# A decoder block with a product-key expert layer on one core: the low halves of split operands issued later, the high halves earlier, part of the one-hot scaling on another engine, and more gathered rows in the first expert product

## The chip, the cores and the metric

One NeuronCore of one Trainium2 chip runs the whole program in one launch. The metric is device microseconds of that core, the median of several runs.

## The reference, cut to what matters

```
x = x + (sigmoid(gate_a) * conv_branch + sigmoid(gate_b) * attention_branch) @ w_out
h = rmsnorm(x)                                   # 512 tokens x 1024
q = h @ peer_wq                                  # 8 heads x two halves of 128
s1, s2 = scores of the two halves against 128 keys each
top 16 of each half, the 256 sums, their top 16  # 16 experts per head and token
experts = e1 * 128 + e2                          # 128 of 16384 experts per token
gates = softmax of the 16 scores
out = sum over the 128 experts: gelu(h . u[expert]) * gate * v[expert]
return rmsnorm(x + out)
```

Everything is float32, and the result has to hold float32 accuracy.

## The kernel before, in words

The kernel multiplies in TensorE's rounded float32 format. Every operand is split in two: a high half, rounded by ScalarE (a copy into that format), and a low half, which is operand minus high half, by VectorE. `mm3` then issues three matmuls for each product: low x high, high x low, high x high.

The program runs in stages; the two of this change are the last two, the **expert products**. For 384 of the 512 tokens (three tiles of 128) the kernel doesn't gather experts. It computes all 16384 of them densely, in 128 blocks of 128 experts:

- **First product** (`u_block`, one call for each block b): `pu[b]` (128 x 1024) times the 384 normalised tokens `hden`, 24 matmuls of 384 columns, then a gelu by ScalarE out of PSUM into `gel`, which is stored to HBM as `Sd` two blocks at a time (the last eight blocks stay on chip as `kept`).
- **Second product** (the last loop over b): `pv[b]` times the weighted gelu values, 18 matmuls of 512 columns into six PSUM banks that stay open for all 128 blocks. For each pair of blocks `a_pair` reloads `Sb` from HBM, VectorE multiplies it by the dense gate matrix `G`, and the product is split into `ah` (ScalarE) and `al` (VectorE).

For the remaining 128 tokens the experts are gathered: for each of 128 slots, POOL gathers one row of `pu` for each token (an indirect DMA of 128 rows x 4 KB) and VectorE takes a dot product (`gathered`, 128 "dots" rows); then 128 rows of `pv` follow, each of which VectorE scales and adds into `x`. These 256 **rows** run beside the two products: so many in the first, the rest spread evenly over the second.

Beside the first product runs the **routing**, all of it background work on VectorE: `level1` (top 16 of every key score, `top16`, five instructions for each of 64 lists), `level2` (candidate sums, their top 16, the expert numbers; one call for each tile of 128 tokens, with round trips through ScalarE), and `scatter` (for the three dense tiles: one-hot matrices by comparison, which PE multiplies into the gate matrix `G`, 16 groups of 8 tokens for each tile). A group needs an `ohs` tile with four parts: a one-hot of the second key (part 0), of the first key (part 1), part 1 times the high half of the gate (part 2, VectorE), and part 1 times the low half (part 3, eight small ScalarE copies with a scale, L1067). PE's 16 small matmuls for a group are queued by `later` behind some block and evicted by two ScalarE copies (`gst`, L1079).

Three things set the order of the work around the change. The engines' queues are written out in program order: nothing reorders them. The weights come through `pump`: three raw buffers (`WRAW`), four split pairs (`WSPL`). `next_w`, called at the start of block b, flushes what is pending (it issues the high and the low half of block b+2's weight), starts a raw load (SP's queue), and leaves block b+3's weight pending. And the background work after each block of the first product is dealt out in nominal microseconds: `bgrun` runs the routing until `U_DVE - U_BG` is spent (`U_DVE` alone until the first tile's experts are known; `U_SC` more when a group of matmuls was queued), then the rows until `U_BG` is spent.

```
        while state["split"] < min(n_split, len(stream)):
            ...
            pend.append([stream[i][1], lo, raw, hi, 0, 0])
```

```
        room = U_DVE
        if len(later) > busy:
            later.pop(0)()
            room += U_SC
        share = U_BG if ready else 0.0
        busy = bgrun(room - share, bgr)
        more = busy or later
        if ready:
            bgrun(share if more else U_END, bgg)
```

The lines that the text below names: L127 and L131 are `flush` (high half `whi` on ScalarE, low half `wlo` on VectorE), L141 the raw load, L172 to L174 the three matmuls, L1110 a dots row, L1116 a row of the second kind, L1151 the gelu, L1192 the multiplication by `G`, L206 and L208 the two halves `ah` and `al` in `split`.

## Time and profile before

| | us |
|---|---|
| median of 3 runs (lowest to highest) | 1809.54 (1803.93 to 1812.57) |
| the profiled execution | 1810.52 |
| its span, first to last instruction | 1808.5 |
| PE busy | 1767.8 |
| VectorE (DVE) busy | 1507.4 |
| ScalarE (ACT) busy | 877.3 |
| DMA, over the span | 239 GB/s |
| first expert product (PE, 126 blocks) | 671 to 1257 |
| second expert product (PE) | 1257 to 1799 |

Matmuls are pipelined, so the time that PE is "busy" covers gaps of up to the length of one matmul: how fast a stage runs is read from the distance between two starts. An engine's wait is put down to the one that released it last. Idle time of an engine that nobody waits for costs nothing.

### The profile page before, as it was taken

To read this page: it belongs to the slowest core of one execution; us is meant where nothing else is said; L and a number is where in the kernel's file an instruction comes from. 1 tells how busy PE (TensorE), PEld (TensorE's weight loads), DVE (VectorE), ACT (ScalarE), POOL (GpSimd) and SP (SyncE) were. 2 spreads that over 40 slices of the span, in tenths; PEclk is the share of its full clock that TensorE was granted. 3 is DMA by queue.
4 is the path that set the end of the run, shared out by engine and by line. 5 is a ranking of instruction groups with operands and counts; after the bars stand their busy time and mean duration, and the time that the engine had idled before them with its cause. 6 is when DMAs were issued, how large, how long until landed. Compare 5 with 4: busy or idle time off the path is not lost.

```text
span 1808.5 us, 25395 instructions
## 1 busy us (share of the span) xinstructions
PE 1767.8 (98%) x9289; PEld 1538.4 (85%) x9289; DVE 1507.4 (83%) x2649; ACT 877.3 (49%) x1622; POOL 388.0 (21%) x303
## 2 busy tenths in 40 slices
PE   8999999999999999999999999999999999999997
PEld 7887777788888889999999999999787787787786
DVE  5799999998755699999888987766888888888887
ACT  5665665535524323344488499953333333333333
POOL 0000000000000000023322322143443444454440
PEclk9999999999999999999999999999999999999999
DMA  6332222122343125578989899999999999999994
GB/s 224 97 94 72 86 76 80 61 82 93 117 148 129 63 78 161 180 250 286 312 277 319 313 314 320 318 355 408 369 384 382 372 385 380 378 384 373 373 335 147
DMA packets 164477, 432.92 MB, mean 239 GB/s; under 512 B 13696, under 2 KB 63488, under 8 KB 162304
## 3 DMA queue, kind: packets, MB, share of 16 engines
q1 hardware_dynamic: 111840, 239.37, 38.5%
q0 software_dynamic: 39424, 138.43, 21.6%
q10 hardware_dynamic: 13088, 53.50, 7.8%
q8 instruction: 73, 1.20, 0.3%
q14 instruction: 52, 0.43, 0.1%
HBM read 376.20 MB, written 50.86 MB: 236 GB/s over the span
## 4 chain that ended last, share of the span: by engine, by line
PE 50%; DVE 22%; ACT 12%; DMA 10%; issue 5%; ACTq 0%; POOL 0%; SPq 0%; POOLq 0%; DVEq 0%
PE mm L172 15%; PE mm L173 15%; PE mm L174 15%; DMA wraw<-in_pv 7%; DVE wlo L131 5%; DVE x L1116 5%; DVE y L498 5%; ACT whi L127 4%; ACT ohs L1067 2%; DMA wraw<-in_pu 2%; ACT ah L206 2%; DVE Sb L1192 2%; PE pvp L1076 2%; DVE grow L1110 2%; DVE ptl L637 1%
## 5 line engine op out<-in xcount | busy, mean ns | idle before, releaser
L131 DVE TENSOR_TENSOR wlo<-wraw,whi 128x1024 fp32r<-128x1024 f32 (+1 forms) x434 | 432.8, 1005 | 101.3 <-ACT whi L127 97.1
L127 ACT ACTIVATE whi<-wraw 128x1024 fp32r<-128x1024 f32 (+1 forms) x429 | 373.7, 893 | 94.6 <-DMA wraw<-in_pv 38.8
L172 PE MATMUL mm<-h2h,wlo 128*128 128x384 f32 (+1 forms) x1152 | 397.8, 345 | 2.1 <-DVE wlo L131 1.6
L173 PE MATMUL mm<-h2l,whi 128*128 128x384 f32 (+1 forms) x1152 | 392.8, 341 | 0.5 <-DVE h2l L208 0.5
L174 PE MATMUL mm<-h2h,whi 128*128 128x384 f32 (+1 forms) x1152 | 393.0, 341 | 0.0
L1097 POOL DMA_INDIRECT grow<-in_pur,sx x128 | 179.1, 1399 | 613.8 <-DVE grow L1110 369.1
L1097 POOL DMA_INDIRECT grow<-in_pv,sx x128 | 185.9, 1452 | 230.1 <-DVE x L1116 203.4
L172 PEld LDWEIGHTS mm<-h2h,wlo 128*128 128x128 f32 x1152 | 216.8, 188 | 7.6 <-DVE wlo L131 2.0
L173 PEld LDWEIGHTS mm<-h2l,whi 128*128 128x128 f32 x1152 | 217.1, 188 | 5.7 <-DVE h2l L208 1.1
L174 PEld LDWEIGHTS mm<-h2h,whi 128*128 128x128 f32 x1152 | 216.8, 188 | 5.3
L173 PE MATMUL mm<-wlo,ah 128*128 128x512 f32 x512 | 203.4, 397 | 9.4 <-DVE wlo L131 9.0
L172 PE MATMUL mm<-whi,al 128*128 128x512 f32 x512 | 199.9, 390 | 0.2 <-DVE al L208 0.2
L174 PE MATMUL mm<-whi,ah 128*128 128x512 f32 x512 | 199.7, 390 | 0.0
L206 ACT ACTIVATE ah<-Sb 128x768 fp32r<-128x768 f32 x60 | 50.8, 846 | 303.9 <-DVE Sb L1192 254.5
L498 DVE SCALAR_TENSOR_TENSOR y<-z,cw,y 128x512 f32<-128x512 f32 x240 | 174.2, 749 | 1.1 <-ACT y L495 0.2
L1116 DVE SCALAR_TENSOR_TENSOR x<-grow,dots,x 128x1024 f32<-128x1024 f32 x128 | 164.5, 1285 | 1.1
L172 PE MATMUL mm<-hTh,wlo 128*128 128x512 f32 x384 | 161.3, 420 | 3.2 <-DVE qa L570 1.7
L1110 DVE SCALAR_TENSOR_TENSOR grow<-grow,hd 128x1024 f32<-128x1024 f32 x128 | 155.0, 1217 | 0.7 <-DMA grow<-in_pur,sx 0.7
L174 PE MATMUL mm<-hTh,whi 128*128 128x512 f32 x384 | 150.6, 392 | 0.0
L173 PE MATMUL mm<-hTl,whi 128*128 128x512 f32 x384 | 150.0, 391 | 0.0
L1151 ACT ACTIVATE gel<-mm 128x384 f32<-128x384 f32 x118 | 57.7, 489 | 182.4 <-PE mm L174 110.1
L173 PEld LDWEIGHTS mm<-wlo,ah 128*128 128x128 f32 x512 | 96.0, 188 | 41.9 <-DVE wlo L131 23.0
(284 smaller groups left out, 2943.9 us busy)
## 6 DMA issues: line engine op xcount, KB each, us to landing
wraw<-in_pu SPq DMA_DIRECT2D x128, 512.0 KB, 4.9
wraw<-in_pv SPq DMA_DIRECT2D x128, 512.0 KB, 6.4
wraw<-in_w_ct SPq DMA_DIRECT2D x48, 512.0 KB, 3.5
Gd<-gst SPq DMA_DIRECT2D x24, 1024.0 KB, 9.8
G<-Gd ACTq DMA_DIRECT2D x16, 1536.0 KB, 10.0
Sb<-Sd ACTq DMA_DIRECT2D x60, 384.0 KB, 6.6
Sd<-gel SPq DMA_DIRECT2D x59, 384.0 KB, 6.1
wraw<-in_w_q SPq DMA_DIRECT2D x16, 512.0 KB, 3.5
```

Source lines behind the costliest of these rows:

```text
L127: nc.scalar.activation(hi[:, nh * q:hi_to * q], raw[:, nh * q:hi_to * q], AF.Copy)
L131: eng.tensor_tensor(lo[:, c], raw[:, c], hi[:, c].bitcast(F32), op=ALU.subtract)
L172: nc.tensor.matmul(o, ll, rh, start=first, stop=False)
L173: nc.tensor.matmul(o, lh, rl, start=False, stop=False)
L174: nc.tensor.matmul(o, lh, rh, start=False, stop=last)
L206: nc.scalar.activation(hi, src, AF.Copy, scale=1.0 if scale is None else scale)
L498: dve.scalar_tensor_tensor(acc, z[:, w:w + S], cw[:, j, w:w + 1], acc, op0=ALU.mult, op1=ALU.add)
L1067: nc.scalar.activation(o[:, 3, g, :, t], o[:, 1, g, :, t], AF.Copy, scale=gl32[:, t0 + u:t0 + u + 1])
L1097: pool.indirect_dma_start(out=t, out_offset=None, in_=src, in_offset=bass.IndirectOffsetOnAxis(ap=sx[:, n % NG:n % NG + 1], axis=0))
L1110: yield 1.25, dve.scalar_tensor_tensor(t, t, 1.0, hd, op0=ALU.mult, op1=ALU.mult, accum_out=dots[:, k:k + 1])
L1116: yield 1.28, dve.scalar_tensor_tensor(o, t, dots[:, k:k + 1], o, op0=ALU.mult, op1=ALU.add)
L1151: nc.scalar.activation(gel[c][:, n, :], p[:, :TD], AF.Gelu_apprx_tanh)
```

## The change

Six edits, all in the two expert products:

- `u_block` calls `flush(4, 0)` after its matmuls and ahead of its gelu: the high half of the weight that this block's `next_w` left pending (block b+3's) is issued there on ScalarE; its low half stays for the next `next_w`, behind this block's background work on VectorE.
- The second product calls `flush(4, 0)` right after `next_w`, to the same effect.
- In `a_pair` the low half `al` is no longer issued right behind the high half: it is put on a list, which the second product's loop runs (`a_low`) after this block's rows.
- In `scatter` the low gates are also stored in float16 (`et` has a fourth part), and one VectorE product scales the one-hots of the first four of a group's eight tokens; ScalarE keeps the other four copies.
- `U_DVE` goes from 2.9 to 3.2.
- `U_BG` goes from 1.15 to 1.3.

```diff
-U_DVE = 2.9
+U_DVE = 3.2
 U_SC = 0.8
-U_BG = 1.15
+U_BG = 1.3
...
-        et = rt.tile([P, 3, P], F16, tag="et", name="et", bufs=2)
+        et = rt.tile([P, 4, P], F16, tag="et", name="et", bufs=2)
...
+        dve.tensor_copy(et[:, 3, :], gl32)
...
-                for u in range(TB):
+                yield 0.36, dve.tensor_tensor(o[:, 3, :TB // TI // 2], o[:, 1, :TB // TI // 2],
+                                              bc(3)[:, :TB // TI // 2], op=ALU.mult)
+                for u in range(TB // 2, TB):
                     g, t = divmod(u, TI)
                     nc.scalar.activation(o[:, 3, g, :, t], o[:, 1, g, :, t], AF.Copy, scale=gl32[:, t0 + u:t0 + u + 1])
...
         p = proj(hden, False)
+        flush(4, 0)
         nc.scalar.activation(gel[c][:, n, :], p[:, :TD], AF.Gelu_apprx_tanh)
...
-        split(hi, lo, a)
+        nc.scalar.activation(hi, a, AF.Copy)
         As[k] = (hi, lo)
+        apend.append(lambda: dve.tensor_tensor(lo, a, hi.bitcast(F32), op=ALU.subtract))
+
+    apend = []
+
+    def a_low():
+        while apend:
+            apend.pop(0)()
...
         if b == NK - KEEP * SB2 + 4:
             a_pair(0)
+            a_low()
...
         hi, lo = next_w()
+        flush(4, 0)
         ah, al = As[c]
         if b == 0:
             left = 2 * NG - ngath[0]
         while 2 * NG - ngath[0] > left * (NK - 5 - b) // (NK - 4):
             if next(bgg, None) is None:
                 break
+        a_low()
```

Three places show how the instructions move. The first is VectorE in the second product, two pairs of blocks (`Sb` is the multiplication by `G`, `al` the low half of that pair, `wlo` the low half of a weight, `x` a gathered row). Before:

```order
L1192 TENSOR_TENSOR Sb<-Sb,G 128x768
L208 TENSOR_TENSOR al<-Sb,ah 128x768
L131 TENSOR_TENSOR wlo<-wraw,whi 128x1024
L1116 SCALAR_TENSOR_TENSOR x_4729<-grow,dots,x_4729 128x1024
L131 TENSOR_TENSOR wlo<-wraw,whi 128x1024
L1116 SCALAR_TENSOR_TENSOR x_4729<-grow,dots,x_4729 128x1024 x2
L1192 TENSOR_TENSOR Sb<-Sb,G 128x768
L208 TENSOR_TENSOR al<-Sb,ah 128x768
```

and now:

```order
L1196 TENSOR_TENSOR Sb<-Sb,G 128x768
L131 TENSOR_TENSOR wlo<-wraw,whi 128x1024
L1119 SCALAR_TENSOR_TENSOR x_4729<-grow,dots,x_4729 128x1024 x2
L1201 TENSOR_TENSOR al<-Sb,ah 128x768
L131 TENSOR_TENSOR wlo<-wraw,whi 128x1024
L1119 SCALAR_TENSOR_TENSOR x_4729<-grow,dots,x_4729 128x1024
L1196 TENSOR_TENSOR Sb<-Sb,G 128x768
```

Between the multiplication that feeds `ah` and the subtraction that reads it stood nothing; now a weight's low half and at least one row stand there. Over the whole program 13 of the 256 rows have moved ahead of the second product's loop: 95 stand there before, 108 now, so the loop has 161 and then 148.

The second place is VectorE in the first product during `level1`, from one weight's low half to the next but one. Before (nine instructions of routing for one weight):

```order
L131 TENSOR_TENSOR wlo<-wraw,whi 128x1024
L908 MAX v<-sc_5948 128x8
L909 MAX_INDEX ix<-v,sc_5948 128x8
L910 MATCH_REPLACE sc_5948<-v,sc_5948 128x128
L911 MAX v<-sc_5948 128x8
L912 MAX_INDEX ix<-v,sc_5948 128x8
L908 MAX v<-sc_5948 128x8
L909 MAX_INDEX ix<-v,sc_5948 128x8
L910 MATCH_REPLACE sc_5948<-v,sc_5948 128x128
L911 MAX v<-sc_5948 128x8
L131 TENSOR_TENSOR wlo<-wraw,whi 128x1024
```

and now (two whole lists, ten instructions):

```order
L131 TENSOR_TENSOR wlo<-wraw,whi 128x1024
L908 MAX v<-sc_5949 128x8
L909 MAX_INDEX ix<-v,sc_5949 128x8
L910 MATCH_REPLACE sc_5949<-v,sc_5949 128x128
L911 MAX v<-sc_5949 128x8
L912 MAX_INDEX ix<-v,sc_5949 128x8
L908 MAX v<-sc_5949 128x8
L909 MAX_INDEX ix<-v,sc_5949 128x8
L910 MATCH_REPLACE sc_5949<-v,sc_5949 128x128
L911 MAX v<-sc_5949 128x8
L912 MAX_INDEX ix<-v,sc_5949 128x8
L131 TENSOR_TENSOR wlo<-wraw,whi 128x1024
```

The first tile's experts are ready three blocks earlier, and the last group of the scatter stands one block earlier.

The third place is ScalarE during the scatter (`ohs` the scaled one-hots, `gel` the gelu, `gst` a group's eviction). Before:

```order
L1067 ACTIVATE ohs<-ohs,gl_9810 128x128 x8
L127 ACTIVATE whi<-wraw 128x1024
L1151 ACTIVATE gel<-mm 128x384
L1079 ACTIVATE gst<-pvp 128x128x4 x2
L1067 ACTIVATE ohs<-ohs,gl_9810 128x128 x8
```

and now:

```order
L1070 ACTIVATE ohs<-ohs,gl_9650 128x128 x4
L127 ACTIVATE whi<-wraw 128x1024
L1155 ACTIVATE gel<-mm 128x384
L1082 ACTIVATE gst<-pvp 128x128x4 x2
L1070 ACTIVATE ohs<-ohs,gl_9650 128x128 x4
```

A group has half the copies. The high half stands in the same place, but it is that of the weight one block further on. PE gets two groups behind the same block at 7 places before and at 4 now.

## Rows read from the trace of the kernel before

**Rows 1.** The page's first part: busy time of each engine, its share of the span, and the number of instructions.

```profile
PE 1767.8 (98%) x9289; PEld 1538.4 (85%) x9289; DVE 1507.4 (83%) x2649; ACT 877.3 (49%) x1622; POOL 388.0 (21%) x303
```

**Rows 2.** Busy time of each engine in stretches of the span: the stretch, its length, then busy time and number of instructions of PE, PE's weight loads, DVE, ACT and POOL, the granted TensorE clock as a share of 2.4 GHz, the mean busy share of the 16 DMA engines, and GB/s. The first two are the two products.

```profile
671.00:1257.00 586.00, 578.20 (x3816) 569.98 (x3815) 488.89 (x1082) 361.99 (x768) 135.58 (x98) 1.00 0.86 289
1257.00:1808.50 551.50, 532.54 (x2306) 429.20 (x2304) 472.69 (x476) 182.88 (x209) 232.03 (x162) 1.00 0.94 356
1040.00:1200.00 160.00, 155.20 (x1220) 149.91 (x1219) 126.44 (x182) 147.99 (x382) 34.19 (x28) 0.99 0.99 318
1200.00:1250.00 50.00, 48.37 (x280) 48.05 (x279) 27.60 (x37) 16.05 (x23) 18.98 (x15) 1.00 1.03 406
1262.00:1750.00 488.00, 478.81 (x2072) 385.67 (x2071) 422.42 (x416) 161.65 (x175) 217.06 (x150) 1.00 0.99 375
```

**Rows 3.** The timeline of PE in the second product: start and length in us, engine, line, operation, tiles and shapes. The first matmul of the product, two matmuls seven starts apart within a block, and the last matmul of the program.

```profile
1257.05 0.39 PE L172 MATMUL mm<-whi,al 128*128 128x512 f32 x1
...
1405.01 0.39 PE L172 MATMUL mm<-whi,al 128*128 128x512 f32 x1
...
1406.60 0.39 PE L173 MATMUL mm<-wlo,ah 128*128 128x512 f32 x1
...
1798.74 0.39 PE L174 MATMUL tp<-whi,ah 128*128 128x512 f32 x1
```

**Rows 4.** What PE waited for, in the first product (the first two rows, 675 to 1262 us) and in the second (the last row, 1262 us to the end): us in total, times, the longest.

```profile
PE pvp L1076 <- ACT gst L1079: 6.2, 13, 2.2
PE mm L172 <- DVE wlo L131: 1.6, 1, 1.6
...
PE mm L173 <- DVE wlo L131: 9.0, 21, 0.7
```

**Rows 5.** What DVE waited for in the second product (1262 to 1790 us), in the same form.

```profile
DVE al L208 <- ACT ah L206: 61.1, 63, 1.2
DVE wlo L131 <- ACT whi L127: 8.3, 9, 1.8
```

**Rows 6.** The timeline of DVE over one pair of blocks of the second product; in brackets the idle time ahead and what ended it.

```profile
1499.77 0.95 DVE L1192 TENSOR_TENSOR Sb<-Sb,G 128x768 f32<-128x768 f32 x1
1501.68 0.96 DVE L208 TENSOR_TENSOR al<-Sb,ah 128x768 fp32r<-128x768 f32 x1 [0.96 <-ACT ah L206]
1502.63 1.23 DVE L131 TENSOR_TENSOR wlo<-wraw,whi 128x1024 fp32r<-128x1024 f32 x1
1503.78 1.28 DVE L1116 SCALAR_TENSOR_TENSOR x<-grow,dots,x 128x1024 f32<-128x1024 f32 x1
...
1507.30 0.95 DVE L1192 TENSOR_TENSOR Sb<-Sb,G 128x768 f32<-128x768 f32 x1
```

**Rows 7.** PE in the first product: the first matmuls of blocks 5 and 6, from the timeline; the group of all small matmuls of the scatter (busy time, mean ns, idle time ahead); and the one of the 48 groups of 16 that waited longest, from the timeline.

```profile
684.95 0.33 PE L172 MATMUL mm<-h2h,wlo 128*128 128x384 f32 x1
...
689.11 0.33 PE L172 MATMUL mm<-h2h,wlo 128*128 128x384 f32 x1
...
L1076 PE MATMUL pvp<-ohs 128*128 128x128 f16 x768 | 52.9, 219 | 6.2 <-ACT gst L1079 6.2
...
1113.18 1.10 PE L1076 MATMUL pvp<-ohs 128*128 128x128 f16 x16 [2.25 <-ACT gst L1079]
```

**Rows 8.** The timeline of ACT over one block of the scatter (rows merged: x8 is eight copies).

```profile
941.43 1.04 ACT L127 ACTIVATE whi<-wraw 128x1024 fp32r<-128x1024 f32 x1
942.38 0.47 ACT L1151 ACTIVATE gel<-mm 128x384 f32<-128x384 f32 x1
942.75 1.06 ACT L1079 ACTIVATE gst<-pvp 128x512 f32<-128x512 f32 x2
943.70 2.49 ACT L1067 ACTIVATE ohs<-ohs,gl 128x128 f16<-128x128 f16 x8
946.04 1.05 ACT L127 ACTIVATE whi<-wraw 128x1024 fp32r<-128x1024 f32 x1
```

**Rows 9.** The timeline of DVE in level 1: the first weight's low half that `next_w` issues there (block 5's), and two starts of a list's first MAX8, with the low half ahead of the first.

```profile
679.73 1.23 DVE L131 TENSOR_TENSOR wlo<-wraw,whi 128x1024 fp32r<-128x1024 f32 x1 [1.23 <-ACT whi L127]
...
721.02 1.21 DVE L131 TENSOR_TENSOR wlo<-wraw,whi 128x1024 fp32r<-128x1024 f32 x1
722.14 0.29 DVE L908 MAX8 v<-sc 128x8 f32<-128x128 f32 x1
...
723.86 0.28 DVE L908 MAX8 v<-sc 128x8 f32<-128x128 f32 x1
```

**Rows 10.** What DVE waited for in the first product, 675 to 1200 us.

```profile
DVE wlo L131 <- ACT whi L127: 46.0, 36, 3.5
DVE sm L1020 <- ACT scv L1018: 9.1, 4, 3.2
DVE gl L1049 <- ACT et L1048: 4.6, 2, 3.3
```

**Rows 11.** Two groups of DVE's instructions between 905 and 1200 us: a dots row, and the float16 product of a one-hot by the high gates (the nearest to the new one, which has half its elements): count, busy time and mean ns of one.

```profile
L1110 DVE SCALAR_TENSOR_TENSOR grow<-grow,hd 128x1024 f32<-128x1024 f32 x55 | 66.9, 1217 | 0.0
L1063 DVE TENSOR_TENSOR ohs<-ohs,et 128x1024 f16<-128x1024 f16 x48 | 33.1, 690 | 1.2
```

**Rows 12.** The page's DMA issues for the weights of the first product (count, KB each, median us from issue to landing), and the longest wait of ACT for one, from its timeline.

```profile
wraw<-in_pu SPq DMA_DIRECT2D x128, 512.0 KB, 4.9
...
1233.76 1.06 ACT L127 ACTIVATE whi<-wraw 128x1024 fp32r<-128x1024 f32 x1 [5.17 <-DMA wraw<-in_pu]
```

## The prediction

> **What bounds the kernel now.** The page calls PE busy for 98% of the span [rows 1], which would leave almost nothing to win. But overlapping matmuls count as busy through short gaps, so I first cut the span at the two products [rows 2] and then read starts, not busy time.
>
> In the second product, seven starts within a block lie 1406.60 - 1405.01 = 1.59 us apart, 0.227 us for each [rows 3]. Its 2304 matmuls (128 blocks of 18) would take 2304 x 0.227 = 523.3 us at that pace; from the first start to one pitch after the last they take 1798.74 + 0.23 - 1257.05 = 541.9 us. So **18.6 us are lost in the second product**. Recorded waits show half of it, 9.0 us in 21 pieces, all for a weight's low half [rows 4]; a short idle time hides behind the matmul before it.
>
> In the first product a block takes 689.11 - 684.95 = 4.16 us [rows 7]. 126 of these are 524.2 us, and 48 groups of the scatter at 1.10 us [rows 7] are 52.8, together 577.0 of the stretch's 586.0 us [rows 2]. **9.0 us are lost in the first product**; the recorded waits name 6.2 us for evictions and 1.6 us for one low half [rows 4].
>
> Nothing ahead of these two stages is touched. So no version of this change can win more than 27.6 us, and the question is which of it comes back, and what is late next.
>
> In the second product VectorE sets the pace. It has 63 waits of 0.96 us, 61.1 us in all, for `ah`, and nothing else of weight [rows 5]. One pair of blocks shows why [rows 6]: the multiplication ends at 1500.7, ScalarE makes `ah`, and the subtraction that VectorE has next can only start at 1501.68. A pair with two rows takes 1507.30 - 1499.77 = 7.5 us, one with three 1.2 to 1.3 us more; PE's pair is 36 x 0.227 = 8.17 us. With 161 rows over 123 blocks, 2.6 for each pair, VectorE needs about 8.3 us: a little more than PE. PE runs out of low halves whenever a three-row pair comes.
>
> **Second product: the low half `al` later, 13 rows fewer.** The wait goes: between the multiplication and the subtraction stand now a low half (1.2 us) and at least one row (1.28 us), over twice the 0.96 us that `ah` needs [rows 6]. That is 0.96 us of VectorE's time for each pair; `al` itself is needed a whole pair later. 13 rows fewer are 13 x 1.2 = 15.6 us more. VectorE's pair falls from 8.3 to about 7.1 us, over 1 us under PE's. Even the rows alone would do: 541.9 - 15.6 = 526.3. The earlier `whi` here only takes ScalarE out of the way of the next low half. What stays are weights that land late: 8.3 us of VectorE's waits were for a `whi` without its raw weight [rows 5]. With 1 us of slack for each pair about half of that should still reach PE. **I take 14 of the 18.6 us back**, between 8 (all of these waits count, and some more) and 18.6.
>
> **Scatter: half of the low copies to VectorE.** A block with one group costs ScalarE 946.04 - 941.43 = 4.6 us, of which eight copies are 2.35 [rows 8]; PE's is 4.16 + 1.10 = 5.3. So ScalarE was only late where two groups met: at the places with two groups behind one block, and once for 2.25 us [rows 7]. Four copies fewer save it 1.2 us for each group. VectorE pays one float16 product of half the size of L1063, 0.69 us [rows 11]: 0.35 us as an estimate, at most 0.69, for each of 48 groups, 17 us in all; it has room there, 126 us busy of 160 [rows 2], so this costs PE nothing. If that room went, it would be at most 17 us. Of the 6.2 us, the 2.25 go, and 4 of the 7 double places stay with their share of the rest: (6.2 - 2.25) x 4/7 = 2.3 us. So 3.9 us come back, between 0 and 6.2.
>
> **High halves one block earlier.** Before, block b+3's high half stood on ScalarE behind block b's gelu, so VectorE waited for it 36 times, 46.0 us [rows 10], mostly in the scatter. This lead is what PE ran out of at the one wait of 1.6 us [rows 4], where raw weights came late by up to 5.17 us [rows 12]. I count the 1.6 us as back (0 at worst). What it may cost: ScalarE's gelu and evictions now queue behind a copy whose weight is asked for one block (4.2 to 5.3 us) sooner, with 4.9 us from issue to landing [rows 12]. An extra wait there reaches PE only through the eviction of a group. Three raw buffers keep the load some two blocks ahead, so I take nothing for it.
>
> **`U_DVE` and `U_BG`: where I expect a loss.** In level 1 VectorE now does two whole lists for each weight: 2 x (723.86 - 722.14) + (722.14 - 721.02) = 4.56 us [rows 9], against PE's 4.16. It falls back 0.40 us with every block, for about 24 blocks. What it has in hand at block 5 is the start of that block on PE [rows 7] less the end of its low half [rows 9], 684.95 - 680.96 = 4.0 us, and the 1.23 us wait that the earlier high half takes away [rows 9]: 5.2 us, gone after 13 blocks. The other 11 cost PE 0.40 each, 4.4 us. Behind that comes level 2, whose round trips through ScalarE (9.1 and 4.6 us of VectorE's idle time [rows 10]) were covered by that lead. There a block costs VectorE 1.9 of routing, 1.04 rows of 1.2 us and a low half of 1.12, 4.2 us: no lead is built up again before the scatter. **I take a loss of 5 us**, between 0 (the lead is longer than I read it) and 18 (4.4 and all of the 13.7).
>
> **The sum**, against the profiled execution of 1810.52 us: -14 - 3.9 - 1.6 + 5 = -14.5, so 1796.0. That execution lies 1.0 us over the median of the runs shown, so I predict **1795 us**. With the ends of all terms: -18.6 - 6.2 - 1.6 = -26.4 gives 1783; -8 + 18 gives 1819.5, which no one mechanism brings together.
>
> **Rivals.** *The DMA engines become the bound* (0.19). They are 0.99 busy from 1262 to 1750 us, 0.99 from 1040 to 1200 and 1.03 from 1200 to 1250 [rows 2]. In the second product this speaks for it, but the rows that leave pay for the higher pace: a row is 0.524 MB, at 375 GB/s 1.4 us, so 488 x 0.99 - 13 x 1.4 = 465 us of transfers stand in a stretch that PE could do in 471. In the first it is worse: about half of the 13 rows fall where the engines are full already, some 8 us. If those 8 us show, and the evictions and late weights with them (0 for both terms), the sum is -14 + 5 + 8 = -1 and the time 1808; if only part of it does, about 1803. It decides once a weight takes longer to land than the three raw buffers look ahead. Against it: VectorE waited for a gathered row nowhere in [rows 5] or [rows 10].
>
> The Trainium skill (DMA: Bandwidth & Descriptors, section Where 436 GB/s comes from) goes further: for transfers between HBM and SBUF a per-core limit of about 358 GB/s binds. By that figure, as an estimate, (488 x 375 GB/s - 6.8 MB) / 358 GB/s = 492 us for a stretch that now takes 488: no gain at all in the second product, and some 1810. This trace disagrees: it moved 375 GB/s over that stretch and 406 GB/s in another [rows 2], and the measurement decides; of the 0.19 this stricter limit has 0.01.
>
> *VectorE becomes the bound of the whole routing* (0.10): the lead at block 5 isn't there, every one of 24 blocks costs 0.40 us, 9.6, and every round trip counts, 13.7. Then 23.3 take the place of 5, and -14 - 5.5 + 23.3 = +3.8 gives 1813, **slower than before**. It decides at block 5: with less than a few us in hand. For it speaks that VectorE and PE took the same time for a block so far; against it, the removed waits.
>
> *Nearly all of it comes back* (0.14): the lead covers the routing; 1787.
>
> My own case, 1790 to 1801, has 0.52. What is left, 0.05, is a loss that I don't see.
>
> **How the numbers follow.** Half a per cent, 9 us, is about what a measurement of this kernel can tell from no change: under 1800.5 counts as faster, over 1818.6 as slower. Faster: nearly all of my own case (0.48), the good case (0.14), a little of the DMA case (0.03): 0.65. Slower: 0.02 of the routing case, 0.04 of the rest: 0.06. The same: 0.29. The range runs from 1784 (all terms at their good ends) to 1809 (the DMA case whole); beyond it lie the routing case and the rest.
>
> **What would show it.** Right: VectorE's wait for `ah` under 10 us in the second product and PE's starts there 524 to 529 us from first to last; ScalarE's copies 192 instead of 384; PE's wait for evictions under 4 us. The loss in the routing: PE waiting for low halves between 740 and 900 us, some 5 us, which it never did before. Wrong: PE waiting for low halves behind `whi` behind a raw weight, in both products (the DMA case), or over 15 us of waits ahead of the scatter (the routing case).

## The result and the profile after

The changed kernel takes **1793.98 us** (median of 8 runs) against 1809.48 for the one before: a ratio of 0.9915, 95% interval 0.9902 to 0.9929, or 15.5 us less. The profiled execution of it took 1794.1 us with a span of 1792.1, 16.4 us under the span of before. The forecast was 1795. The total came out right, but not all of its terms did; the experiments show which.

The page's first part, to be held against [rows 1]: TensorE is again "98% busy", in a span that is 16 us shorter, so this share tells nothing here.

```profile
PE 1758.9 (98%) x9289; PEld 1541.4 (86%) x9289; DVE 1523.9 (85%) x2700; ACT 834.7 (47%) x1430; POOL 407.7 (23%) x303
```

The stretches of the changed kernel, in the columns of [rows 2]: the first product, the second with the end of the program, the longer part of the scatter, the middle of the second product, and 7 us around one wait that is new.

```profile
671.00:1258.00 587.00, 579.21 (x3818) 569.91 (x3818) 524.70 (x1167) 314.29 (x576) 180.39 (x113) 0.99 0.87 301
1258.00:1792.10 534.10, 522.63 (x2305) 432.16 (x2303) 453.53 (x443) 187.07 (x208) 206.89 (x147) 1.00 0.92 353
1035.00:1194.00 159.00, 157.41 (x1247) 152.48 (x1246) 144.10 (x225) 112.48 (x251) 54.29 (x34) 1.00 1.03 351
1262.00:1750.00 488.00, 487.76 (x2152) 403.99 (x2153) 428.71 (x408) 172.25 (x182) 202.84 (x142) 1.00 0.98 376
794.00:801.00 7.00, 4.94 (x16) 4.94 (x17) 6.79 (x21) 1.06 (x1) 3.36 (x2) 0.51 0.75 276
```

The first product is as long as it was. The second starts 0.84 us later than before and is 17 us shorter; in its middle PE is busy for 487.76 of 488 us (478.81 before, [rows 2]). These are its first and last matmul on PE's timeline, against [rows 3]:

```profile
1257.89 0.39 PE L172 MATMUL mm<-whi,al 128*128 128x512 f32 x1
...
1782.35 0.39 PE L174 MATMUL tp<-whi,ah 128*128 128x512 f32 x1
```

From the first start to the end of the last matmul that is 524.8 us (542.1 before, reckoned the same way), against 523.3 for 2304 matmuls at 0.227.

What PE waited for in the first product (675 to 1262 us, the first three rows) and from there to the end (the last), against [rows 4]:

```profile
PE mm L172 <- DVE wlo L131: 5.8, 2, 5.6
PE pvp L1079 <- ACT gst L1082: 1.4, 2, 0.7
PE pvp L1079 <- issue: 0.5, 2, 0.2
...
PE mm L172 <- ACT kept L1155: 2.1, 1, 2.1
```

The 21 waits of the second product are gone, and so are 11 of the 13 for evictions. In their place stand one of 5.6 us in the first product and one of 2.1 us at the border.

**The wait of 5.6 us.** VectorE's timeline around it, at block 30. The two rows in brackets wait for gathers that POOL had only issued at 784.41 and 785.78, when the first tile's experts became known, and the low half that PE needs stands behind both:

```profile
789.27 1.23 DVE L1113 SCALAR_TENSOR_TENSOR grow<-grow,hd 128x1024 f32<-128x1024 f32 x1 [1.46 <-DMA grow<-in_pur,sx]
790.42 0.08 DVE L1113 DVE_READ_ACCUMULATOR grow<-grow,hd 128x1 f32 x1
793.64 1.22 DVE L1113 SCALAR_TENSOR_TENSOR grow<-grow,hd 128x1024 f32<-128x1024 f32 x1 [3.13 <-DMA grow<-in_pur,sx]
794.79 0.08 DVE L1113 DVE_READ_ACCUMULATOR grow<-grow,hd 128x1 f32 x1
794.79 1.22 DVE L131 TENSOR_TENSOR wlo<-wraw,whi 128x1024 fp32r<-128x1024 f32 x1
```

The low half that PE waits for ends at 796.01. PE's row there:

```profile
796.06 0.69 PE L172 MATMUL mm<-h2h,wlo 128*128 128x384 f32 x1 [5.55 <-DVE wlo L131]
```

The row's nominal cost is 1.25. With `U_BG` at 1.15 a block takes one row when it starts afresh; at 1.3 one row leaves 0.05, and a second is dealt in the same block, here before either had landed. Even a single row came too early in the kernel before; it waited 0.7 us, and that line of the view stands below those that [rows 10] shows:

```profile
DVE grow L1110 <- DMA grow<-in_pur,sx: 0.7, 1, 0.7
```

The first row of the changed kernel waited 1.46 us, the second 3.13. The matmul takes 0.69 us instead of 0.33, and the granted clock from 794 to 801 us is 0.51: the lower level, 1.2 GHz. The records have it from 794.06, while PE still stood, to 800.89 us, so 4.8 us of it fell on PE at work.

**The wait of 2.1 us.** ScalarE around the border. The last gelu (`kept`) stands behind the early high half of a weight that had not landed:

```profile
1260.75 1.06 ACT L127 ACTIVATE whi<-wraw 128x1024 fp32r<-128x1024 f32 x1 [6.33 <-DMA wraw<-in_pv]
...
1261.71 0.47 ACT L1155 ACTIVATE kept<-mm 128x384 f32<-128x384 f32 x1
```

VectorE's waits in the second product (1262 to 1790 us), against [rows 5]:

```profile
DVE al L1201 <- ACT ah L1199: 36.2, 35, 2.6
DVE al L1201 <- issue: 13.0, 9, 1.4
DVE wlo L131 <- ACT whi L127: 11.5, 8, 3.3
```

These three add up to 61 us, against the 69 of [rows 5], but for another reason. `ah` now waits on ScalarE for PE, where before it waited for VectorE's multiplication (254.5 us, 51 times). ScalarE's waits in the same stretch begin with:

```profile
ACT ah L1199 <- PE tp L174: 171.4, 59, 3.0
```

So VectorE is ahead, and PE does not lose by its waits.

### The profile page after: what moved, and what is told of

Read it like the earlier page. It is cut to its first block, busy times and chain, and to the rows that moved or that the text cites. A ratio compares the mean times of both kernels' runs of the same rounds, so it can differ in the third digit from the quotient of the medians.

```text
span 1792.1 us, 25332 instructions
## 1 busy us (share of the span) xinstructions
PE 1758.9 (98%) x9289; PEld 1541.4 (86%) x9289; DVE 1523.9 (85%) x2700; ACT 834.7 (47%) x1430; POOL 407.7 (23%) x303
## 4 chain that ended last, share of the span: by engine, by line
PE 64%; DVE 23%; DMA 7%; ACT 4%; issue 2%; POOL 0%; SPq 0%; POOLq 0%; ACTq 0%; DVEq 0%
PE mm L172 17%; PE mm L173 17%; PE mm L174 17%; DVE wlo L131 5%; DVE y L498 5%; DMA wraw<-in_pu 5%; PE tp L173 3%; PE tp L174 3%; PE tp L172 3%; PE pvp L1079 2%; DVE ix L909 1%; DVE sc L910 1%; DVE ix L912 1%; DVE ptl L637 1%; DVE v L911 1%
## 5 line engine op out<-in xcount | busy, mean ns | idle before, releaser
L127 ACT ACTIVATE whi<-wraw 128x1024 fp32r<-128x1024 f32 (+1 forms) x429 | 378.6, 894 | 336.7 <-DMA wraw<-in_pu 133.5
L131 DVE TENSOR_TENSOR wlo<-wraw,whi 128x1024 fp32r<-128x1024 f32 (+1 forms) x434 | 432.5, 1004 | 64.0 <-ACT whi L127 59.6
L1100 POOL DMA_INDIRECT grow<-in_pur,sx x128 | 202.8, 1584 | 546.6 <-DVE grow L1113 312.0
L1100 POOL DMA_INDIRECT grow<-in_pv,sx x128 | 181.9, 1421 | 252.9 <-DVE x L1119 232.4
L173 PE MATMUL mm<-wlo,ah 128*128 128x512 f32 x512 | 199.3, 389 | 0.0
L172 PEld LDWEIGHTS mm<-whi,al 128*128 128x128 f32 x512 | 96.1, 188 | 22.4 <-ACT kept L1155 2.5
L174 PEld LDWEIGHTS mm<-whi,ah 128*128 128x128 f32 x512 | 96.1, 188 | 20.0
```

The costliest lines, as they stand in the source:

```text
L127: nc.scalar.activation(hi[:, nh * q:hi_to * q], raw[:, nh * q:hi_to * q], AF.Copy)
L131: eng.tensor_tensor(lo[:, c], raw[:, c], hi[:, c].bitcast(F32), op=ALU.subtract)
L172: nc.tensor.matmul(o, ll, rh, start=first, stop=False)
L173: nc.tensor.matmul(o, lh, rl, start=False, stop=False)
L174: nc.tensor.matmul(o, lh, rh, start=False, stop=last)
L1100: pool.indirect_dma_start(out=t, out_offset=None, in_=src, in_offset=bass.IndirectOffsetOnAxis(ap=sx[:, n % NG:n % NG + 1], axis=0))
```

## The experiments

A stage's length is read from PE's timeline: the first product from the first matmul of block 2, the second from its first matmul to the end of the last. The ratios stand against the kernel before on the same chip (medians 1807.2 to 1808.5 us). Kernels measured on different chips are best compared by these ratios, which can move a difference by some 2 us. Lengths come from the profiled execution, which can lie some us off the median; a wait at the border of the two products falls into the one or the other column.

| kernel | time, us | ratio [95%] | first | second |
|---|---|---|---|---|
| before | 1809.48 | 1 | 586.0 | 542.1 |
| after | 1793.98 | 0.9915 [0.9902, 0.9929] | 586.7 | 524.8 |
| e3 before + early high halves | 1803.49 | 0.9979 [0.9966, 0.9991] | 583.6 | 538.9 |
| e2 before + `al` later | 1854.82 | 1.0259 [1.0240, 1.0279] | 585.6 | 587.1 |
| e10 before + both, second product only | 1794.85 | 0.9927 [0.9907, 0.9947] | 586.6 | 526.4 |
| e7 before + the two constants | 1815.61 | 1.0045 [1.0026, 1.0063] | 607.6 | 526.9 |
| e1 after, `al` in its old place | 1799.65 | 0.9954 [0.9940, 0.9968] | 587.7 | 528.0 |
| e6 after, eight copies | 1808.71 | 0.9999 [0.9983, 1.0015] | 604.8 | 522.4 |
| e4 after, first row later | 1785.70 | 0.9876 [0.9854, 0.9897] | 579.1 | 523.0 |
| e5 e4 without the last early high half | 1785.41 | 0.9873 [0.9850, 0.9896] | 585.3 | 522.4 |
| e14 e4 without early high halves in the first product | 1786.35 | 0.9884 [0.9865, 0.9902] | 580.1 | 524.0 |
| e8 after, old constants | 1787.92 | 0.9894 [0.9873, 0.9914] | 576.5 | 528.0 |
| e12 e8 without the last early high half | 1784.28 | 0.9876 [0.9856, 0.9895] | 579.1 | 523.5 |
| e11 e8 without early high halves in the first product | 1787.32 | 0.9890 [0.9872, 0.9909] | 576.2 | 528.3 |

### The second product: which part freed it

**e1**, the changed kernel with `al` back behind `ah`:

```
-        nc.scalar.activation(hi, a, AF.Copy)
+        split(hi, lo, a)
         As[k] = (hi, lo)
-        apend.append(lambda: dve.tensor_tensor(lo, a, hi.bitcast(F32), op=ALU.subtract))
```

> The changed kernel with one edit undone: the low half al stands again right behind ah, so VectorE waits 0.96 us for each pair of the second product. My theory: the 13 rows that moved and the wait are two ways to the same slack, and the rows alone (15.6 us of VectorE's time) bring VectorE's pair from 8.3 to about 8.05 us, under PE's 8.17; PE's starts in the second product then span some 526 to 530 us (541.7 in the kernel before, 524.5 in the changed one) and the time is 1794 to 1799 us. Rival: the deferred al is what brought the gain; without it VectorE still runs with no lead, PE waits for low halves at each three-row pair, the span there is over 535 us and the time over 1803 us.

**e2**, the kernel before with only that edit the other way, `al` issued behind the block's background rows:

```
-        split(hi, lo, a)
+        nc.scalar.activation(hi, a, AF.Copy)
         As[k] = (hi, lo)
+        apend.append(lambda: dve.tensor_tensor(lo, a, hi.bitcast(F32), op=ALU.subtract))
...
             if next(bgg, None) is None:
                 break
+        a_low()
```

> The kernel before with one edit alone: al is issued after the rows. All 161 rows stay in the second product, and nothing changes in the first. My theory: VectorE's pair falls from 8.3 to 7.3 us, PE becomes the bound there, its starts span 524 to 528 us, and the time is 1793 to 1797 us. Rival (the DMA engines bind at a share of 1.0): the transfers of the second product stay 0.99 x 488 = 483 us in a stretch that PE could do in 471, so only some 5 us come back, the DMA share stays at 0.99 or over while VectorE waits for high halves whose weights land late, and the time is 1803 to 1806 us.

**e3**, the kernel before with only the early high halves of both products:

```
         p = proj(hden, False)
+        flush(4, 0)
...
         hi, lo = next_w()
+        flush(4, 0)
         ah, al = As[c]
```

> The kernel before with one edit alone: the high half of a weight is issued one block earlier in both products. My theory: it takes away VectorE's 46 us of waits for high halves in the first product, but PE lost only 1.6 us to them; in the second product VectorE still waits for ah, and PE still loses about 18 us. At the border of the two products the last gelu stands behind a high half whose weight lands late, which costs PE 2 to 4 us. Together 1807 to 1812 us. Rival: the earlier high half is what freed the second product; then the time is under 1800 us.

e1 gave 1799.65, 0.65 us over my theory's range. Of the 18.6 us of the second product only 3.2 are lost again, although VectorE is back at waiting for `ah` in every pair (71.9 us in 63 pieces). e3 gave 5 us (4 by the ratio), between my theory and the rival, and missed both. **e2 was a clear miss**: 46 us slower, where both theories had it faster. VectorE and ScalarE over one pair of e2 (from the timeline, other engines left out) show why; the row to look at is the one in brackets on L131:

```profile
1507.07 0.95 DVE L1192 TENSOR_TENSOR Sb<-Sb,G 128x768 f32<-128x768 f32 x1
1508.11 0.85 ACT L1195 ACTIVATE ah<-Sb 128x768 fp32r<-128x768 f32 x1 [6.97 <-DVE Sb L1192]
1508.86 1.04 ACT L127 ACTIVATE whi<-wraw 128x1024 fp32r<-128x1024 f32 x1
1509.94 1.23 DVE L131 TENSOR_TENSOR wlo<-wraw,whi 128x1024 fp32r<-128x1024 f32 x1 [1.91 <-ACT whi L127]
...
1511.08 1.28 DVE L1116 SCALAR_TENSOR_TENSOR x<-grow,dots,x 128x1024 f32<-128x1024 f32 x1
1512.28 0.95 DVE L1197 TENSOR_TENSOR al<-Sb,ah 128x768 fp32r<-128x768 f32 x1
1513.14 1.22 DVE L131 TENSOR_TENSOR wlo<-wraw,whi 128x1024 fp32r<-128x1024 f32 x1
```

What VectorE has next after the multiplication is now a low half. Its high half stands on ScalarE behind `ah`, and `ah` waits for that very multiplication. So VectorE waits for two copies instead of one: 1.9 us in a pair instead of 0.96. In the second product of e2 (1262 to 1790 us) it waited 111.4 us in 59 pieces, and PE waited for `al` (to 1850 us). Of VectorE:

```profile
DVE wlo L131 <- ACT whi L127: 111.4, 59, 2.0
```

And of PE:

```profile
PE mm L172 <- DVE al L1197: 49.1, 38, 2.2
```

VectorE was the pacer, so each of these us counts. From 1300 to 1750 us it is busy for 355.02 of 450 us, 7.2 us of a pair of 587.1 / 64 = 9.17; with 1.9 of wait that is 9.1.

**e10** tests this: before, with the deferred `al` of e2, and in the second product alone the early high half:

```
         hi, lo = next_w()
+        flush(4, 0)
         ah, al = As[c]
```

> The kernel before with two edits in the second product only: the low part of the activations is asked after the background work, and each block's weight high half is asked right after the block's weights are taken, ahead of the activations. Theory A (a loop through ScalarE): with the low part alone deferred, VectorE's weight low half waited 1.9 us in each of 58 pairs for a high half that stood on ScalarE behind ah, which stood behind VectorE's product with the gate; asking the high half a block earlier breaks that loop. Then VectorE waits in the second product for neither, the second product runs at 227 ns per matmul (523 us, no PE wait over 2 us), and the time is 1809 - 18 = 1789 to 1793 us. Rival B (71 rows still gathered in the second product make VectorE the bound whatever the order): the second product keeps 8 us or more of PE waits on VectorE, 1799 to 1806 us. Rival C (deferring the low part is itself what costs): near 1850 us as with the low part alone.

One line turns 1854.82 into 1794.85, 2 us over theory A's range. The second product takes 526.4 us, 2.1 of it one wait at the border, and VectorE's waits for high halves there fall from 111.4 us in 59 pieces (e2) to 12.5 in 9. **Shown: with the rows of before, the two edits give their gain only together** (e3 alone: 3.2 us of the stage; e2 alone: a loss of 45; both: a gain of 15.7). That the early high half takes the copy out of the loop over `ah` fits these waits. The two edits alone give as much as the whole change.

**e7** asks for the third way, fewer rows: the kernel before with `U_DVE = 3.2` and `U_BG = 1.3` and nothing else:

```
-U_DVE = 2.9
+U_DVE = 3.2
-U_BG = 1.15
+U_BG = 1.3
```

> The kernel before with the two constants alone (3.2 and 1.3). Theory A, in two terms. Second product: VectorE's cycle per pair of blocks there is 8.46 us, with 0.97 us of wait for ah in it, and 31 rows x 1.22 us over 64 pairs take 0.59 us off it: 7.87 us, less than PE's 36 x 0.227 = 8.17, so PE's losses there go (-17 to -19 us) with low and high parts where they were. First product: eight copies per piece of the scatter at the faster rate, and the two first rows in one block, as in the changed kernel with eight copies (604.8 us against 586): +15 to +19 us. Sum 1805 to 1811 us, with the two terms seen apart in the profile. Rival B (the order of the low parts is what holds the second product, not how much VectorE has to do): the second product keeps its losses, 1822 to 1828 us.

The second product takes 526.9 us: theory A, and B falls. VectorE's waits for `ah` are all still there (60.8 us, 63 times), and PE loses only some 4 us. The 31 rows in this expectation and in that of e8 are a miscount of mine: a row is two instructions in the trace (the row and the read of its accumulator). The 71 rows of e10's expectation are wrong too: 161 rows of both kinds stand in that loop. 35 dots rows start in the second product before, 20 after the change and 19 in e7. A row holds VectorE for 1.15 us (793.64 to 794.79 at block 30). 16 x 1.15 = 18.4 us, 0.29 for each pair, bring VectorE's 542.1 / 64 = 8.47 down to 8.18, just PE's 8.17. So **either cure was enough for the second product**, and the change holds both. The price lies in the other stage: 607.6 us, 21.6 more than before, over the 15 to 19 that I gave it, and so the time missed the expected range by 5 us.

### The first product: where as much went as came

**e6**, the changed kernel with eight ScalarE copies again:

```
-        et = rt.tile([P, 4, P], F16, tag="et", name="et", bufs=2)
+        et = rt.tile([P, 3, P], F16, tag="et", name="et", bufs=2)
...
-        dve.tensor_copy(et[:, 3, :], gl32)
...
-                yield 0.36, dve.tensor_tensor(o[:, 3, :TB // TI // 2], o[:, 1, :TB // TI // 2],
-                                              bc(3)[:, :TB // TI // 2], op=ALU.mult)
-                for u in range(TB // 2, TB):
+                for u in range(TB):
```

> The changed kernel with all eight low one-hot copies on ScalarE again (no VectorE half product). Theory A (the half product is what took the waits off the scatter's evictions): PE's waits for the evictions come back to 5 to 6 us in some 13 pieces as with the early high half alone (5.4 us), 1797 to 1800 us. Rival B (the half product only trades ScalarE for VectorE time, 96 x 0.3 us, and the waits went because the routing ends at another place): within 2 us of the changed kernel, 1792 to 1796 us.

It gave 1808.71, the whole gain of the change back, far outside both theories, which had this part at no more than 6 us. PE's waits in e6, from 675 us to the end of the first product:

```profile
PE pvp L1076 <- ACT gst L1079: 10.9, 18, 3.6
PE mm L172 <- DVE wlo L131: 7.3, 3, 5.0
```

And in e7, which has eight copies as well (675 to 1262 us):

```profile
PE pvp L1076 <- ACT gst L1079: 14.3, 19, 2.5
PE mm L172 <- DVE wlo L131: 7.9, 5, 5.3
```

Two things come together. ScalarE is busy for 144.42 of 156 us of the scatter before (1044 to 1200) and for 112.48 of 159 after, so with eight copies a delay finds little idle time to go into. The stretch of before, in the columns of [rows 2]:

```profile
1044.00:1200.00 156.00, 151.20 (x1196) 146.06 (x1194) 122.44 (x176) 144.42 (x372) 32.51 (x27) 0.99 1.00 322
```

The half product also has a nominal cost of 0.36 of its own, by which fewer groups are dealt to a block. Counting runs of 32 small matmuls on PE (two groups behind one block) gives 7 such places before, 9 in e6 and e7, 4 after, 2 in e8: the constants make more, the half product makes fewer. No run tells the shorter copies from the fewer double places. A wait also costs more than its length when PE's clock falls with it. In e6 the records have the lower clock for 3.4 us at each of three places beside block 30, two at an eviction and one at a low half (before: one).

**e8**, the changed kernel with the constants of before:

```
-U_DVE = 3.2
+U_DVE = 2.9
-U_BG = 1.3
+U_BG = 1.15
```

> The changed kernel with the two constants of the first product as before (2.9 and 1.15), so some 30 rows of the gather go back into the second product; early high halves, deferred low parts and the VectorE half product stay. Theory A (the second product has the room): 31 rows x 1.22 us = 38 us of VectorE work come back into a stage where VectorE waited 60 of 524 us; PE stays at 227 ns per matmul there, VectorE's lead in the first product is not used up (over 3 us at block 22, no 5.5 us wait at block 30), and the time is 1783 to 1788 us, as with the first row later. Rival B (the moved rows are what frees the second product): PE waits of 8 us or more in the second product, 1793 to 1802 us.

1787.92, at the upper edge of theory A: 6 us under the whole change by the medians, 4 by the ratios, whose intervals overlap. The stages show it better. The first product takes 576.5 us; in the middle of the second (1300 to 1750 us) PE is busy for 450.00 of 450. It waits 3.7 us at the border. So the rows need not move: the 16 rows more, some 18 us, fit into the second product once its order is right, and moving them costs 10.2 us in the first.

**e4** deals the first row two blocks later. In `gathered`, ahead of the first row:

```
+            if n == 0:
+                yield 2.6, None
             t = rows.pop(0)
```

> The changed kernel with one edit added: when the first tile's experts are known, the first gathers are issued at once, but the first dots row is dealt out two blocks later. In the changed kernel's trace VectorE meets the first two rows 4.6 us before they have landed, in one block, with no lead left; PE stands still for 5.55 us and then runs 6.8 us at half the clock. My theory: this is the whole of the loss in the routing that counts, and 5.5 + 3.4 = 9 us come back: 1784 to 1787 us, with no idle time of PE over 2 us before 900 us. Rival: VectorE has simply too much work in the routing, and the wait only shows up elsewhere; then PE loses the same 5 us to other low halves there and the time stays 1791 to 1795 us.

1785.70, as expected: 8.3 us under the changed kernel, 7 by the ratios. The first product falls from 586.7 to 579.1 us, 7.6 us: the wait of 5.55, and half of the 4.8 us that PE worked at the lower clock, make 8.0. (The expectation lets PE run all 6.8 us at that clock; 2 of them lie in the wait.) VectorE's rows at the same place now have no gather ahead of the low halves; two rows still come in one block, but when they come, both have landed:

```profile
785.45 1.21 DVE L131 TENSOR_TENSOR wlo<-wraw,whi 128x1024 fp32r<-128x1024 f32 x1
...
788.46 1.21 DVE L131 TENSOR_TENSOR wlo<-wraw,whi 128x1024 fp32r<-128x1024 f32 x1
...
791.45 1.22 DVE L131 TENSOR_TENSOR wlo<-wraw,whi 128x1024 fp32r<-128x1024 f32 x1
...
794.40 1.21 DVE L1115 SCALAR_TENSOR_TENSOR grow<-grow,hd 128x1024 f32<-128x1024 f32 x1
...
795.53 1.22 DVE L1115 SCALAR_TENSOR_TENSOR grow<-grow,hd 128x1024 f32<-128x1024 f32 x1
796.68 0.08 DVE L1115 DVE_READ_ACCUMULATOR grow<-grow,hd 128x1 f32 x1
796.68 1.22 DVE L131 TENSOR_TENSOR wlo<-wraw,whi 128x1024 fp32r<-128x1024 f32 x1
```

So it is not two rows in a block that cost PE, but rows dealt ahead of their gathers. The constants bring the wait (5.25 us in e7, none in e8). How much of it is the second row's no run shows; as an estimate, without that row the low half would have come some 4.4 us sooner (790.42 instead of 794.79), so most of it.

### The early high half of the first product

**e5** is e4, **e12** is e8, each with this; **e11** and **e14** are e8 and e4 with the `flush` of `u_block` left out in every block.

```
-        flush(4, 0)
+        if b < NK - 1:
+            flush(4, 0)
```

> The changed kernel with the first row of the gather dealt one step later, and without the early high half in the last block of the first product, whose gelu stood behind a copy that waited for its raw weight. Theory A: the 2.1 us wait of PE at the border to the second product is gone as far as the late first row has left it (0.2 us of it is left there), so 1783.5 to 1786 us, the same as with the later row alone. Rival B (the copy's place matters by itself): 2 us under it, 1781.5 to 1783.5 us; or, the other way, the second product starts with a wait for its own first high half of 1 to 2 us, 1787 us.

> The changed kernel with the two constants as before (2.9 and 1.15) and without the early high half in the last block of the first product. With the constants alone put back PE waited 3.7 us at the border for the last gelu, which stood on ScalarE behind a high half whose raw weight came late, and ran at half clock for some us after it. Theory A: that wait goes, and the half clock with it: 4 to 6 us under the 1788 of that kernel, 1782 to 1785 us. Rival B: the second product's own first low half is then late by as much, 1786 to 1790 us.

> The same without the early high half in any block of the first product: low parts deferred and high halves early in the second product, the VectorE half product, the constants as before. Theory A (in the first product the early high half is no gain: it puts gelus and evictions on ScalarE behind copies that wait for late raw weights, and VectorE has room for the waits that it spares): 1781 to 1786 us, not over the kernel with it in all blocks but the last. Rival B (it is what took VectorE's 46 us of waits for high halves off the routing): the routing ends later, PE waits for low halves, 1788 to 1794 us.

> The changed kernel with the first row of the gather dealt one step later (1785.6 us) and without the early high half in the first product. The constants (3.2 and 1.3) leave VectorE no room in the routing's blocks: its lead there is used up at block 22. Theory A: VectorE then pays for every wait for a high half, PE waits for low halves in the blocks of the first routing and of the scatter, 1790 to 1800 us. Rival B (the early high half does nothing in the first product): 1783 to 1787 us.

e5 stays at e4's time, as A had it. e12 came at 1784.28, in A's range, but its interval overlaps e8's. e11 (1787.32) has a border wait as long as e8's, only for the high half itself: it falls between A and B. e14 (1786.35) fits B, and A's 1790 to 1800 is out. So leaving it out changes nothing that these runs can tell: **with the half product in, the early high half of the first product is worth nothing measurable**. The border is short of weights either way. PE's waits there in e11 (675 to 1265 us):

```profile
PE mm L172 <- ACT whi L127: 4.1, 1, 4.1
```

What it can cost shows in e5's profiled execution, 3.6 us over its median. ScalarE there, in the scatter:

```profile
1067.04 1.06 ACT L127 ACTIVATE whi<-wraw 128x1024 fp32r<-128x1024 f32 x1 [4.26 <-DMA wraw<-in_pu]
1068.00 0.47 ACT L1158 ACTIVATE gel<-mm 128x384 f32<-128x384 f32 x1
1068.37 1.07 ACT L1082 ACTIVATE gst<-pvp 128x512 f32<-128x512 f32 x2
```

One late weight, and gelu and evictions stand behind it; PE waited 5.28 us for them, and the records have the lower clock for 6.8 us, 5 of them behind the wait.

e12 and e4 take 1784 to 1786 us, 8 to 10 us less than the changed kernel (7 by the ratios, and the intervals lie apart); which of the two is better can't be told from these runs.

## Why the prediction was right, and which of its steps were not

**Second product, -14: right, too small.** It gave 17.2 us (542.1 to 524.8), most of the 18.6. The late weights, for which I had kept some 4 us, cost PE nothing but the 2.1 us at the border: VectorE waited 11.5 us for high halves, and was far enough ahead. "Even the rows alone would do: 541.9 - 15.6 = 526.3" is what e7 measured, 526.9. (13 rows is right by their place in the program. By the time at which they start it was 15, and 16 in e7.) The sign that I had named for this term failed: VectorE's wait for `ah` was to be under 10 us, and it is 36.2, because PE now holds ScalarE back. The other signs came: PE's starts span 524.5 us, ScalarE's copies are 192, and PE waited 1.4 us for evictions. Wrong in the working: "**The earlier `whi` here only takes ScalarE out of the way of the next low half.**" It is the condition for the deferral, which alone costs 46 us (e2). I had looked at what `al` waits for and not at what stands next in VectorE's queue once `al` has left its place.

**Scatter, -3.9: the place was right, the size wrong.** The waits for evictions fell from 6.2 to 1.4 us, 4.8 us of my 6.2 at most. But the part is worth 10.4 us in the first product without the constants (e10 to e11: 586.6 to 576.2) and 18 with them (e6 to after: 604.8 to 586.7). Of the 10.4, recorded waits make 6.8 and the lower clock 1.7 (half of 3.4 us); where the rest was lost no row shows. I had counted the double places of one order (7 and 4) as if they came from the copies. They came from two parts at once, which pull apart: with the old constants the half product brings them to 2. And I had priced a wait at its length, without the clock behind it. Its cost on VectorE was as said, 0.42 us for a product (0.35 estimated), and hidden.

**Early high halves, -1.6: about that, and not free.** Alone they shorten the first product by 2.4 us (e3, one execution); with the half product, by nothing measurable (e11, e14). "I take nothing for it" left out the 2.1 us at the border, though without them the border costs PE as much (2.1 us in e10, 4.1 in e11). ScalarE's waits for raw weights in the first product rose from 26.3 us (11 pieces) to 133.5 (63).

**Routing, +5: the sign right, the mechanism half wrong.** From e8 to the changed kernel it is +10.2 us in the first product. My mechanism did happen: the lead on PE falls by 0.39 us a block from 5.4 us at block 5, and is gone at block 22. I had put that at block 18. It cost PE only 1 us up to block 29. Another 7.6 is what no step of mine had: two rows in one block, just when the first tile's experts are known, ahead of their gathers. The remaining 1.6 no run places. A wait of PE for a low half between 740 and 900 us, the sign of this loss, did come (5.6 us), but it came for the gathers and not for the lead. "VectorE waited for a gathered row nowhere in [rows 5] or [rows 10]" holds of the lines shown there, but not of the trace, where the first row waited 0.7 us. That was the hint: with 1.3 a second row comes behind it.

So the sum was right by luck, because **two misses cancelled**: a gain of some 9.5 us in the first product (586.0 to 576.5 with both the high halves and the half product) where I had 5.5, and a loss of 10.2 where I had 5.

**The rivals.** The DMA engines are not the bound: 0.98 busy and 376 GB/s in the middle of the second product, with PE at its pace there, and 0.99 and 387 GB/s in e8. VectorE as the bound of the whole routing: its lead did run out, but for some blocks, not for 24. That nearly all comes back is what e4 and e12 show, some 22 of the 27.6 us: e4 with the rows dealt later, e12 with the old constants.

## What to carry to other kernels

Before an instruction is moved to the back of an in-order queue because it waits, look at what takes its place and trace that one's producers: if they stand behind the same producer, the wait grows. When two edits cure the same loss, time each alone and both: here the order alone did it, and moving the work as well only cost something elsewhere. Compare a dealing constant with the nominal cost of the piece it deals; crossing it changes how many pieces come at once. Then look at the first time they come: here their data was not there yet, and two blocks later the same two pieces cost nothing that can be measured.

## What the runs showed of the hardware beside this

The granted clock fell to its lower level, 1.2 GHz, at some of PE's waits, and not at others as long. From 1.5 us behind the 2.25 us of [rows 7] the records have it there for 3.4 us; e2 has a wait of 2.23 us at the same place and full clock after it, and so has the changed kernel at its 2.1 us at the border. At the 5.55 us of block 30 and the 5.28 us of e5 it fell while PE still stood, for 6.8 us each. Taking the 5.55 us wait out gave the first product back 7.6 (e4). And one core moved 376 to 387 GB/s over 450 us and more of the second product without PE losing its pace.
